# Five raw weight places instead of three in the second sweep of the first feed-forward layer, in the room of values that come later, and the work beside it spread over more tiles

## The chip, the core and the metric

The kernel runs on one core of a Trainium2 chip. The metric is the device time of one execution in microseconds. Before the change three runs gave 2960.24, 2964.97 and 2967.89 us; the median is 2964.97 us. The engines are named as in the profile: PE multiplies matrices, DVE works on vectors, ACT computes functions and copies, POOL is the general engine that also issues some of the DMAs here, SP issues the weight loads.

## The reference

A trunk of two layers works on 1024 latent tokens and 256 context tokens of width 1024. Layer 0 mixes tokens with a Conformer convolution module, layer 1 with grouped-query attention (16 heads, 4 key and value heads, head size 64, rotary positions on the latent tokens). A SwiGLU feed-forward of inner width 2816 follows each. What the change touches lies in the feed-forward of layer 0 and the start of layer 1:

```python
hx = rmsnorm(x, norm_g[i, 0]) * (1.0 + sc_x) + sh_x          # shift and scale from silu(c) @ w_mod
...
x = x + g_x * rmsnorm(yx, norm_g[i, 1])
fx = rmsnorm(x, norm_g[i, 2]) * (1.0 + scf_x) + shf_x
x = x + gf_x * rmsnorm(swiglu(fx, ffn_w1[i], ffn_w3[i], ffn_w2[i]), norm_g[i, 3])

def swiglu(h, w1, w3, w2):
    return (jax.nn.silu(h @ w1) * (h @ w3)) @ w2
```

In layer 1, `hx @ wq`, `hx @ wk` and `hx @ wv` give queries, keys and values, and the context tokens give keys and values of their own; queries and keys are normalised per head.

## The kernel before

All arithmetic is in float32. A product is computed from two halves of each operand: a value is rounded to a high half and the remainder is the low half, and three matmuls (high by high, high by low, low by high) are added in PSUM. So each weight block of 128 rows by 1024 columns takes three steps before PE can use it: SP loads it into a *raw place*, ACT rounds it into the high half (L144 or L161), and DVE subtracts to get the low half (L148 or L164). A raw place is free again once DVE has read it for the last time. The raw places are a list, `self.raws`, that `raw()` (L98) goes around. High and low halves have three buffers each (`wh`, `wl`).

The tokens stand in three pieces: C (256 context tokens), L and R (the two halves of the latent tokens, 512 each). The inner width 2816 is cut into 22 tiles of 128, in six groups of 4, 4, 4, 4, 3 and 3 (`GROUPS`).

The feed-forward of layer 0 is done in two sweeps over its weights. The first takes C and L together (L1347), the second R alone (L1393). `ffn` is a generator. For each tile it computes the two inner products and the product with silu (`up` or `up_fast`); after the first tile of a group it adds the down projection of the group before (`w2`, `down`: 96 matmuls of 512 columns for a group of 4); at the end `last` does the last group, with `evict` adding each result from PSUM to the sum in SBUF (L925) and `sq_acc` adding its square to a running sum (L389 on ACT, L390 on DVE).

In the second sweep all tiles but the first go through `up_fast` (L852). It computes a pair of 2 by 2 block products with seven block products instead of eight, each of four steps of three matmuls of 256 columns: 84 matmuls per tile. It takes two raw places for a tile (`r1`, `r3`, L859), issues their loads (L860, L861), and forms the sums and differences of the blocks in place on DVE (`tt`, L879), so that a place is in use from the start of its load until the last of its sums is split (L896). Three steps on ACT copy or silu partial results (L885, L898, L903), others add them on DVE (all L879).

Before the change the second sweep has three raw places: the two of the list, `wr0` and `wr1`, and `self.room()`, a tile named `q` (L1390). The second sweep of layer 1, which runs the same `up_fast` on R, has five.

Beside the second sweep runs a queue of background generators, `bgq`. After each step of the sweep, `pump` adds a credit, and generators run as long as the credit is above zero; each `yield` of a generator takes its cost off. The credit per unit of the sweep's work is set at L1401: 0.2 in the main part and 2.0 in the last group. The background does in this order (`early`, L1376): the last step of C and L of layer 0 (`final`, with its normalisation by L692 and L695), the norm of C into layer 1, keys and values of C (`qkv`, with `qk_pair`), eight steps of the norm of L; and then (`late`) the rest of the norm of L: the sums of squares added over partitions by PE (`stat`, L364), a reciprocal square root on DVE, its spread by PE transposes (L378), and eight applications, each of them L398 on DVE, L403 on ACT and L404 on DVE. Behind the sweep come keys, values and queries of L (`qkv`, L1405), the last step of R (L1409), its norm (L1411), its keys, values and queries (L1415), and attention.

Two large tiles matter for the change. `HR` has 5120 values per partition. During the second sweep its first part still serves C; from `qkv` of C on it holds the values of all heads and tokens (`self.vst`, L1380). Earlier in the kernel it holds inputs and the conditioning row (`cond_row`, L252).

The program is written in the order of these generators; a scheduler then orders the instructions of each engine by priority, which `later` lowers for a few (L362, L377), and each engine does its instructions strictly in that order.

Of the kernel before, what the change touches and what calls it, by code (L numbers as in the profile page):

```python
# [55 lines left out]
class Kern:  # L56
# [193 lines left out]
                                 bias=self.c["bmod"][:, 0, f:f + 1], scale=1.0)  # L250

    def cond_row(self, cr):  # L252
        self.nc.sync.dma_start(cr.rearrange("p s d -> p (s d)"), self.a["crow"].to_broadcast([P, 2048]))
        self.nc.scalar.activation(cr, cr, AF.Silu)

    def mod_dve(self, fs, cr, raws, junk):

        nc = self.nc

        def load(i):  # L260
            if i >= len(fs):
                return None
            raw = raws[i % len(raws)]
            if raw is None:
                raw = self.raw()
            nc.sync.dma_start(raw, self.a["wmodT"][0, fs[i]])
            return raw
        nxt = load(0)
        for i, f in enumerate(fs):
            raw, nxt = nxt, load(i + 1)  # L270
            for s in range(2):
                nc.vector.tensor_tensor_reduce(out=junk, in0=raw, in1=cr[:, s, :], scale=1.0, scalar=0.0,
                                               op0=ALU.mult, op1=ALU.add,
                                               accum_out=self.mod[0][s][:, f:f + 1])
                yield 1.13
        for s in range(2):
            m = self.mod[0][s][:, fs[0]:fs[-1] + 1]
            nc.vector.tensor_tensor(m, m, self.c["bmod"][:, 0, fs[0]:fs[-1] + 1], op=ALU.add)

    def mod_half(self, l, fs, cr, raws, junk):  # L280

        nc = self.nc
        part = self.cp.tile([P, 2, 48], F32, tag="mpart", name="mpart")

        def load(i):
            if i < 2 * len(fs):
                h = i % 2 * 512
                if self.tie is not None:
                    nc.scalar.copy(raws[i % len(raws)][:, 0:1], self.tie[:, 0:1].bitcast(F32))
                nc.gpsimd.dma_start(raws[i % len(raws)], self.a["wmodT"][l, fs[i // 2]][:, h:h + 512])  # L290
        ahead = len(raws) - 1
        for i in range(ahead):
            load(i)
        for i in range(2 * len(fs)):
            f, h = fs[i // 2], i % 2
            load(i + ahead)
            for s in range(1 if l and f >= 16 else 2):
                nc.vector.tensor_tensor_reduce(out=junk, in0=raws[i % len(raws)], in1=cr[:, s, h * 512:h * 512 + 512],
                                               scale=1.0, scalar=0.0, op0=ALU.mult, op1=ALU.add,
                                               accum_out=(part[:, s] if h else self.mod[l][s])[:, f:f + 1])  # L300
# [743 lines left out]
    def qkv(self, h, col0, n, wk, rope=None, highs=()):  # L1044
# [16 lines left out]
        for j in range(n // P):  # L1061
            out = self.bank("mm")
            self.mm3(out,
                     self.pairs(*h, j * P, (j + 1) * P),
                     lambda k: tuple(w[:, (k % 4) * 256:(k % 4 + 1) * 256] for w in wv[k // 4]),
                     KT, 256)
            jj = col0 // P + j
            ov = out[:, :256].rearrange("p (h d) -> p h d", d=HD)
            vh, vl = self.vst[:, :, jj, 0:HD], self.vst[:, :, jj, HD:P]
            nc.scalar.copy(vh, ov)  # L1070
            nc.vector.tensor_tensor(vl, ov, vh.bitcast(F32), op=ALU.subtract)
            yield 0.5
        if rope is not None:
            for t in range(NKV):
                def qsink(i, v):
# [6 lines left out]
                             qsink,  # L1082
                             self.rq[t][:, lat0 // P * 4:(lat0 + n) // P * 4])
                yield 5.0

    def load_k(self, t, kt, c0=0, c1=TOK):
        k = kt.bitcast(F32).rearrange("p (a t) -> p a t", a=2)
# [34 lines left out]
    def values(self, t, Ps, sums, dst, done):  # L1122
        nc, c = self.nc, self.c
        av = self.bank("av")
        for j in range(NJ):
            tp = self.bank("pt")
            for h in range(4):
                nc.tensor.transpose(tp[:, h * P:(h + 1) * P], Ps[h][:, j * P:(j + 1) * P], c["ident"])  # L1128
            ph, pl = self.ptring[self.ptslot % len(self.ptring)]
            self.ptslot += 1  # L1130
            nc.scalar.copy(ph, tp)  # L1131
            nc.vector.tensor_tensor(pl, tp, ph.bitcast(F32), op=ALU.subtract)  # L1132
            with self.later(self.lav):
                nc.tensor.matmul(av, lhsT=self.vst[:, t, j, :], rhs=ph, start=j == 0, stop=False)  # L1134
                nc.tensor.matmul(av, lhsT=self.vst[:, t, j, :], rhs=pl, start=False, stop=j == NJ - 1)  # L1135
            yield 0.87

        r = sums[:, 1, :]
# [46 lines left out]
    def build(self):  # L1185
# [3 lines left out]
        hs = {b: [] for b in PIECES}  # L1189

        nv = CG * OW
        hr = self.T("HR", [P, TOK + nv + 2 * 1024 + 256])
        cr = hr[:, TOK + nv:TOK + nv + 2048].rearrange("p (s d) -> p s d", s=2)
        xs = {"C": hr[:, :KT * CTX].rearrange("p (k n) -> p k n", k=KT), "L": self.T("T6", [P, KT, 512])}

        def load_x(b):
# [51 lines left out]
        self.u = hr[:, :TOK]  # L1248

        self.v = [hr[:, o:o + nv].rearrange("p (g n) -> p g n", g=CG) for o in (TOK, TOK + nv)]  # L1250
        self.vsum = hr[:, TOK + nv + 2048:TOK + nv + 2048 + OW]
        ut = self.T("HS", [P, 2, 2, CG, UW], F32R)
        self.u2 = [ut[:, i] for i in range(2)]
        kt = self.T("KB", [P, CG * UW + CG * NM * PH + 1024])
# [71 lines left out]

        def mods():

            cr = room[:, 2048:4096].rearrange("p (s d) -> p s d", s=2)
            raws = [room[:, o:o + 512] for o in (4096, 4608)]  # L1330
            q = self.room()
            raws += [q[:, :512], q[:, 512:]]
            self.cond_row(cr)
# [7 lines left out]
        def rest_R():  # L1341
            yield from pp("R")
            yield from mods()
        room = self.T("HR", [P, 5120])
        self.bgq.append(rest_R())
        fm, fg = [], None
        for i, us in enumerate(self.ffn(0, [(fv["C"][0], CTX), (fv["L"][0], 512)],  # L1347
# [75 lines left out]
    def attention(self, final, qr):  # L1423
# [50 lines left out]
        def out_proj(q0, otag, tags, ytag, box, xtag):  # L1474
# [18 lines left out]
            more = [self.acc(512), xr[:, KT, :]]  # L1493
            box += [more, xr]
            for k in range(KT):
                o = self.bank("mm")
# [219 lines left out]
```

## Time and profile before

| what | value |
|---|---|
| median of three runs | 2964.97 us |
| the profiled execution's own time | 2966.95 us |
| its span in the trace | 2965.2 us |
| PE busy | 2864.0 us, 97% of the span |
| DVE busy | 2159.8 us, 73% |
| ACT busy | 1331.8 us, 45% |
| PE's mean granted clock | 0.985 of full speed |
| moved by DMA | 336.58 MB, 114 GB/s on the mean |

The second sweep of layer 0 goes from 1071.6 to 1447.1 us, where `last` begins. The seam, as it is called below, goes from there to 1531 us, where the key projection of R begins. The second sweep of layer 1 goes from 2599.8 to 2940 us. PE's busy time is modelled from the starts of its matmuls, so a busy PE is not always a PE at full speed: a stage's length against the number of its matmuls says more. The granted clock is 1.00 at full speed. In rows of waits the columns are the waiting engine and line, what it waited for, then the sum in us, how often, and the longest.

### The profile page before, as it was taken

The numbers are of one execution on the slowest core, as the hardware profiler recorded it, in microseconds if no ns is written. First come the engines' busy times: TensorE is split into PE (matmuls) and PEld (weight loads), VectorE is DVE, ScalarE is ACT, GpSimd is POOL, SyncE is SP. The second block draws the span as 40 slices with busy tenths as digits, with TensorE's granted clock in tenths as the row PEclk, the third lists the DMA queues.
The fourth block names the chain that finished last, engine by engine and source line by source line (L and its number), as shares of the span: only waits on it lengthen the run. The fifth ranks groups of instructions, "written<-read, shape, count | busy, mean of one in ns | idle before, by whom it ended". The sixth has DMA issues, their size and how long they took to land.

```text
span 2965.2 us, 42721 instructions
## 1 busy us (share of the span) xinstructions
PE 2864.0 (97%) x16462; PEld 2452.4 (83%) x16462; DVE 2159.8 (73%) x3746; ACT 1331.8 (45%) x2227; POOL 222.5 (8%) x377
## 2 busy tenths in 40 slices
PE   8999989999999999999999999989999999999998
PEld 6888877888888888898888778767777778889997
DVE  6887787857555387776786899786676756787777
ACT  5222265532222244443444688645555543444444
POOL 0000001011122001000011111100010000010000
PEclk9999999999999999999999999999999999999999
DMA  6443444334355224333445211222223142343332
GB/s 246 133 124 97 122 129 166 114 119 135 125 168 175 66 84 152 100 102 96 138 153 172 88 45 45 93 84 82 63 77 85 56 149 93 114 162 109 103 100 76
DMA packets 131467, 336.58 MB, mean 114 GB/s; under 512 B 31296, under 2 KB 52832, under 8 KB 130112
## 3 DMA queue, kind: packets, MB, share of 16 engines
q1 hardware_dynamic: 77728, 222.33, 24.0%
q0 software_dynamic: 29344, 103.83, 10.7%
q10 hardware_dynamic: 24192, 7.70, 1.1%
q8 instruction: 129, 2.11, 0.3%
q14 instruction: 74, 0.61, 0.1%
HBM read 289.50 MB, written 38.93 MB: 111 GB/s over the span
## 4 chain that ended last, share of the span: by engine, by line
PE 83%; DVE 9%; DMA 3%; ACT 2%; issue 2%; ACTq 0%; POOL 0%; SPq 0%; DVEq 0%; POOLq 0%
PE ps L172 15%; PE ps L173 15%; PE ps L174 15%; PE ps L1110 4%; PE ps L1128 4%; PE ps L874 3%; PE ps L876 3%; PE ps L875 3%; PE ps L453 2%; PE ps L1134 2%; PE ps L455 2%; PE ps L454 2%; PE ps L1135 2%; PE ps L184 1%; PE ps L185 1%
## 5 line engine op out<-in xcount | busy, mean ns | idle before, releaser
L174 PE MATMUL ps<-T,wl 128*128 128x512 f32 (+1 forms) x1360 | 502.1, 369 | 3.0 <-DVE wl L148 3.0
L172 PE MATMUL ps<-T,wh 128*128 128x512 f32 (+1 forms) x1360 | 503.9, 371 | 0.9 <-DVE sm L838 0.4
L173 PE MATMUL ps<-T,wh 128*128 128x512 f32 (+1 forms) x1312 | 483.5, 369 | 0.0
L144 ACT CAST wh<-wr 128x1024 fp32r<-128x1024 f32 (+1 forms) x225 | 233.3, 1037 | 434.7 <-PE ps L173 323.7
L148 DVE TENSOR_TENSOR wl<-wr,wh 128x1024 fp32r<-128x1024 f32 (+1 forms) x225 | 271.5, 1207 | 175.2 <-ACT wh L144 173.8
L874 PE MATMUL ps<-T,wh 128*128 128x256 f32 x1092 | 313.3, 288 | 13.0 <-ACT wh L161 8.3
L876 PE MATMUL ps<-T,wl 128*128 128x256 f32 x1092 | 305.6, 283 | 2.3 <-DVE wl L164 1.9
L875 PE MATMUL ps<-T,wh 128*128 128x256 f32 x1092 | 306.9, 281 | 0.0
L1132 DVE TENSOR_TENSOR T<-ps,T 128x512 fp32r<-128x512 f32 x320 | 216.8, 687 | 108.2 <-ACT T L1131 107.4
L174 PEld LDWEIGHTS ps<-T,wl 128*128 128x128 f32 x1360 | 258.5, 190 | 43.7 <-DVE wl L148 3.3
L172 PEld LDWEIGHTS ps<-T,wh 128*128 128x128 f32 x1360 | 258.5, 190 | 43.2 <-ACT T L1498 1.7
L173 PEld LDWEIGHTS ps<-T,wh 128*128 128x128 f32 x1312 | 249.7, 190 | 38.1 <-DVE T L164 0.7
L1131 ACT CAST T<-ps 128x512 fp32r<-128x512 f32 x320 | 185.9, 585 | 192.3 <-PE ps L1128 178.5
L173 PE MATMUL ps<-HS,wh 128*128 128x512 f32 x656 | 256.7, 391 | 0.0
L172 PE MATMUL ps<-HS,wh 128*128 128x512 f32 x608 | 238.3, 392 | 1.6 <-ACT wh L144 1.6
L174 PE MATMUL ps<-HS,wl 128*128 128x512 f32 x608 | 237.3, 390 | 0.0
L874 PEld LDWEIGHTS ps<-T,wh 128*128 128x128 f32 x1092 | 206.6, 189 | 24.0 <-ACT wh L161 14.1
L876 PEld LDWEIGHTS ps<-T,wl 128*128 128x128 f32 x1092 | 205.8, 190 | 4.8 <-DVE wl L164 4.6
L875 PEld LDWEIGHTS ps<-T,wh 128*128 128x128 f32 x1092 | 207.3, 190 | 0.4
L1128 PE MATMUL ps<-cst,T 128*128 128x128 f32 x1100 | 190.2, 275 | 3.3 <-DVE T L1132 3.3
L1116 DVE TENSOR_SCALAR_CACHE_REDUCE T<-ps,rq 128x1280 f32<-128x1280 f32 x110 | 170.1, 1546 | 27.4 <-PE ps L1110 22.2
L1128 PEld LDWEIGHTS ps<-cst,T 128*128 128x128 f32 x1100 | 133.0, 141 | 49.9 <-DVE T L1132 31.0
(357 smaller groups left out, 6179.3 us busy)
## 6 DMA issues: line engine op xcount, KB each, us to landing
wr<-in_w SPq DMA_DIRECT2D x185, 512.0 KB, 3.6
wr<-in_pw SPq DMA_DIRECT2D x35, 512.0 KB, 3.6
q<-in_w SPq DMA_DIRECT2D x31, 512.0 KB, 3.7
HR<-in_wmodT POOLq DMA_DIRECT2D x56, 256.0 KB, 4.2
q<-in_wmodT POOLq DMA_DIRECT2D x56, 256.0 KB, 3.9
KB<-in_w SPq DMA_DIRECT2D x24, 512.0 KB, 3.6
q<-qsd POOLq DMA_DIRECT2D x32, 256.0 KB, 3.3
wr<-in_wo SPq DMA_DIRECT2D x16, 512.0 KB, 3.6
```

The costliest lines, as they stand in the source:

```text
L144: nc.scalar.copy(hi, raw)
L148: nc.vector.tensor_tensor(lo, raw, hi.bitcast(F32), op=ALU.subtract)
L172: nc.tensor.matmul(out[:, :n], lhsT=wh, rhs=xh, start=k == 0, stop=False)
L173: nc.tensor.matmul(out[:, :n], lhsT=wh, rhs=xl, start=False, stop=False)
L174: nc.tensor.matmul(out[:, :n], lhsT=wl, rhs=xh, start=False, stop=k == nk - 1)
L874: nc.tensor.matmul(out, lhsT=wh, rhs=bh, start=first and k == 0, stop=False, **skip)
L875: nc.tensor.matmul(out, lhsT=wh, rhs=bl, start=False, stop=False, **skip)
L876: nc.tensor.matmul(out, lhsT=wl, rhs=bh, start=False, stop=k == 3, **skip)
L1116: nc.vector.tensor_scalar(out=pt, in0=sc, scalar1=rq[:, h:h + 1], scalar2=None, op0=ALU.mult, op1=ALU.min, accum_out=mn)
L1128: nc.tensor.transpose(tp[:, h * P:(h + 1) * P], Ps[h][:, j * P:(j + 1) * P], c["ident"])
L1131: nc.scalar.copy(ph, tp)
L1132: nc.vector.tensor_tensor(pl, tp, ph.bitcast(F32), op=ALU.subtract)
```

## The change

`HR` shrinks from 5120 to 4096 values per partition, and a new tile `HV` has the other 1024, so the memory in use is the same. The values of the first two token tiles (the context's) go to `HV`, those of the others to `HR`, which `qkv` now claims only when the first latent value is computed, that is after the sweep. In the meantime the last 2048 values per partition of `HR` are two more raw places: the second sweep of layer 0 has five. They are taken off the list after it. The conditioning row, which lay in one piece, is loaded and put through silu in two halves, one of them in `HV`. The credits of the background beside the sweep go from 0.2 to 0.16 in the main part and from 2.0 to 0.65 in the last group. A scratch row of the output projection moves from one tile to `HV`.

```diff
     def cond_row(self, cr):
-        self.nc.sync.dma_start(cr.rearrange("p s d -> p (s d)"), self.a["crow"].to_broadcast([P, 2048]))
-        self.nc.scalar.activation(cr, cr, AF.Silu)
+        for s in range(2):
+            self.nc.sync.dma_start(cr[s], self.a["crow"][:, 1024 * s:1024 * s + 1024].to_broadcast([P, 1024]))
+            self.nc.scalar.activation(cr[s], cr[s], AF.Silu)
...
             jj = col0 // P + j
-            vh, vl = self.vst[:, :, jj, 0:HD], self.vst[:, :, jj, HD:P]
+            if jj >= 2 and len(self.vst) == 1:
+                self.vst.append(self.T("HR", [P, NKV, NJ - 2, P], F32R))
+            vh, vl = self.value(slice(None), jj)[:, :, 0:HD], self.value(slice(None), jj)[:, :, HD:P]
...
+    def value(self, t, j):
+        return self.vst[0][:, t, j, :] if j < 2 else self.vst[1][:, t, j - 2, :]
...
-        hr = self.T("HR", [P, TOK + nv + 2 * 1024 + 256])
-        cr = hr[:, TOK + nv:TOK + nv + 2048].rearrange("p (s d) -> p s d", s=2)
+        hr = self.T("HR", [P, KT * 512])
+        cr = [hr[:, TOK + nv:TOK + nv + 1024], self.T("HV", [P, 1024])]
...
-        self.vsum = hr[:, TOK + nv + 2048:TOK + nv + 2048 + OW]
+        self.vsum = hr[:, TOK + 2 * nv:TOK + 2 * nv + OW]
...
-            cr = room[:, 2048:4096].rearrange("p (s d) -> p s d", s=2)
-            raws = [room[:, o:o + 512] for o in (4096, 4608)]
+            cr = [room[:, 2048:3072], room[:, 3072:]]
+            raws = [half[:, :512], half[:, 512:]]
...
-        room = self.T("HR", [P, 5120])
+        room, half = self.T("HR", [P, 4096]), self.T("HV", [P, 1024])
...
-            self.vst = self.T("HR", [P, NKV, NJ, P], F32R)
+            self.vst = [self.T("HV", [P, NKV, 2, P], F32R)]
...
-        self.raws.append(self.room())
+        self.raws += [self.room(), room[:, 2048:3072], room[:, 3072:]]
...
-            self.pump((0.2 if i < FT + 4 * (len(GROUPS) - 1) else 2.0) * us)
+            self.pump((0.16 if i < FT + 4 * (len(GROUPS) - 1) else 0.65) * us)
+        del self.raws[3:]
...
-            xr = self.T(xtag, [P, KT + 1, 512])
+            xr = self.T(xtag, [P, KT if q0 else KT + 1, 512])
+            last = self.T("HV", [P, 512]) if q0 else xr[:, KT, :]
```

In the rows below, names are `output<-inputs` with buffer numbers, and the changed kernel's lines are shifted by one or two against those of before (L860 is L861, L364 is L365, L390 is L391, L398 is L399, L404 is L405, L925 is L926).

The first place is SP's queue in the second sweep, between the loads of the third and the fourth group of the down projection. Before, consecutive rows:

```order
L860 DMA wr0_73<-in_w1 128x1024
L861 DMA wr1_74<-in_w3 128x1024
L860 DMA q_8799<-in_w1 128x1024
L860 DMA wr1_74<-in_w1 128x1024
L861 DMA wr0_73<-in_w3 128x1024
L860 DMA wr0_73<-in_w1 128x1024
L861 DMA q_8799<-in_w3 128x1024
```

At the same place of the changed kernel:

```order
L861 DMA HR_4326<-in_w1 128x1024
L861 DMA wr1_74<-in_w1 128x1024
L862 DMA wr0_73<-in_w3 128x1024
L862 DMA q_8805<-in_w3 128x1024
L861 DMA HR_4326<-in_w1 128x1024
L143 DMA wr0_73<-in_w2 128x1024
L862 DMA HR_4326<-in_w3 128x1024
```

The loads are the same; the place that each goes into has moved from three names to five (`HR` stands for two of them).

The second place is DVE's order in the seam, at the end of the second sweep. `wl_12537` is the low half of the first latent key weight, `acc_12401` the running sum of squares of R, `T1` the sums of the down projection, and `T2` the low half of the norm of L. Before:

```order
L148 TENSOR_TENSOR wl_12537<-q_8799,wh_12536 128x1024
L390 TENSOR_TENSOR acc_12401<-acc_12401,sb_12423 128x512
L398 SCALAR_TENSOR_TENSOR sb_12426<-T5_4324,col100_7900,ps_72 128x512
L398 SCALAR_TENSOR_TENSOR sb_12430<-T5_4324,col100_7900,ps_72 128x512
L398 SCALAR_TENSOR_TENSOR sb_12434<-T5_4324,col100_7900,ps_72 128x512
L404 SCALAR_TENSOR_TENSOR T2_12381<-sb_12426,mod10_103,T3_12380 128x512
L404 SCALAR_TENSOR_TENSOR T2_12381<-sb_12430,mod10_103,T3_12380 128x512
L404 SCALAR_TENSOR_TENSOR T2_12381<-sb_12434,mod10_103,T3_12380 128x512
```

In the changed kernel the low half of the same weight is `wl_12543`, and it stands here:

```order
L399 SCALAR_TENSOR_TENSOR sb_12500<-T5_4328,col100_7906,ps_72 128x512
L391 TENSOR_TENSOR acc_12401<-acc_12401,sb_12497 128x512
L926 TENSOR_TENSOR T1_8806<-ps_72,T1_8806 128x512
L405 SCALAR_TENSOR_TENSOR T2_12427<-sb_12500,mod10_103,T3_12426 128x512
L399 SCALAR_TENSOR_TENSOR sb_12517<-T5_4328,col100_7906,ps_72 128x512
L391 TENSOR_TENSOR acc_12401<-acc_12401,sb_12514 128x512
L926 TENSOR_TENSOR T1_8806<-ps_72,T1_8806 128x512
L405 SCALAR_TENSOR_TENSOR T2_12427<-sb_12517,mod10_103,T3_12426 128x512
L399 SCALAR_TENSOR_TENSOR sb_12534<-T5_4328,col100_7906,ps_72 128x512
L391 TENSOR_TENSOR acc_12401<-acc_12401,sb_12531 128x512
L148 TENSOR_TENSOR wl_12543<-q_8805,wh_12542 128x1024
```

The low half of the key weight has moved from ahead of the applications of L's norm to behind all but the last step of them, and these now alternate with R's sums instead of standing in runs of three.

The third place is PE's order at the start of the latent key projection, where the matmuls of the sweep's last group end (`HS` is the inner product of R). Before:

```order
L185 MATMUL ps_72<-HS_8801,wl_12397 128x512
L183 MATMUL ps_72<-T3_12380,wh_12536 128x512
L184 MATMUL ps_72<-T2_12381,wh_12536 128x512
L185 MATMUL ps_72<-T3_12380,wl_12537 128x512
L183 MATMUL ps_72<-T3_12380,wh_12541 128x512
L184 MATMUL ps_72<-T2_12381,wh_12541 128x512
L183 MATMUL ps_72<-T3_12380,wh_12536 128x512
```

In the changed kernel:

```order
L185 MATMUL ps_72<-HS_8807,wl_12397 128x512
L183 MATMUL ps_72<-T3_12426,wh_12542 128x512
L184 MATMUL ps_72<-T2_12427,wh_12542 128x512
L183 MATMUL ps_72<-T3_12426,wh_12547 128x512
L184 MATMUL ps_72<-T2_12427,wh_12547 128x512
L172 MATMUL ps_72<-wh_12641,T3_12426 128x256 x2
L365 MATMUL ps_72<-cst_75,acc_12401 128x1 x4
L185 MATMUL ps_72<-T3_12426,wl_12543 128x512
```

The first matmul by a low half of a key weight has moved from third to behind all that doesn't need one, two matmuls of the value projection and the four of R's statistics among it.

More of the change, by code (lines that the diff above doesn't have):

```diff
@@ L271, in mod_dve @@
             for s in range(2):
-                nc.vector.tensor_tensor_reduce(out=junk, in0=raw, in1=cr[:, s, :], scale=1.0, scalar=0.0,
+                nc.vector.tensor_tensor_reduce(out=junk, in0=raw, in1=cr[s], scale=1.0, scalar=0.0,
                                                op0=ALU.mult, op1=ALU.add,
@@ L297, in mod_half @@
             for s in range(1 if l and f >= 16 else 2):
-                nc.vector.tensor_tensor_reduce(out=junk, in0=raws[i % len(raws)], in1=cr[:, s, h * 512:h * 512 + 512],
+                nc.vector.tensor_tensor_reduce(out=junk, in0=raws[i % len(raws)], in1=cr[s][:, h * 512:h * 512 + 512],
                                                scale=1.0, scalar=0.0, op0=ALU.mult, op1=ALU.add,
@@ L1133, in values @@
             with self.later(self.lav):
-                nc.tensor.matmul(av, lhsT=self.vst[:, t, j, :], rhs=ph, start=j == 0, stop=False)
-                nc.tensor.matmul(av, lhsT=self.vst[:, t, j, :], rhs=pl, start=False, stop=j == NJ - 1)
+                nc.tensor.matmul(av, lhsT=self.value(t, j), rhs=ph, start=j == 0, stop=False)
+                nc.tensor.matmul(av, lhsT=self.value(t, j), rhs=pl, start=False, stop=j == NJ - 1)
             yield 0.87
@@ L1488, in out_proj @@
             box.append((y, yacc))
-            xr = self.T(xtag, [P, KT + 1, 512])
+            xr = self.T(xtag, [P, KT if q0 else KT + 1, 512])
+            last = self.T("HV", [P, 512]) if q0 else xr[:, KT, :]
             for q in range(0, KT, 2):
                 nc.gpsimd.dma_start(xr[:, q:q + 2, :], self.x2d[:, q:q + 2, CTX + q0:CTX + q0 + 512])
-            more = [self.acc(512), xr[:, KT, :]]
+            more = [self.acc(512), last]
             box += [more, xr]
```

## The prediction

> **What bounds the kernel now.** The page comes first, for its shares of the span and for the chain of work that ended last.
>
> ```profile
> span 2965.2 us, 42721 instructions
> PE 2864.0 (97%) x16462; PEld 2452.4 (83%) x16462; DVE 2159.8 (73%) x3746; ACT 1331.8 (45%) x2227; POOL 222.5 (8%) x377
> PE 83%; DVE 9%; DMA 3%; ACT 2%; issue 2%; ACTq 0%; POOL 0%; SPq 0%; DVEq 0%; POOLq 0%
> ```
>
> PE bounds the kernel, but only 83% of the chain is PE: 9% is DVE and 3% DMA. So I asked for busy time by stage. The first row is layer 0's second sweep (the stage that changes), the next four are pieces of layer 1's second sweep, which runs the same code with five raw weight places, and the last three are the projection of the context keys inside layer 0's sweep and the two halves of the seam behind it. Columns: length, then busy time and instructions of PE, PEld, DVE, ACT and POOL, the granted clock, the DMA share, GB/s.
>
> ```profile
> 1071.60:1447.10 375.50, 358.28 (x2413) 326.94 (x2412) 289.03 (x495) 166.53 (x259) 16.86 (x28) 0.99 0.36 114
> 2622.00:2652.20 30.20, 28.51 (x230) 27.21 (x228) 29.91 (x49) 16.40 (x26) 2.75 (x5) 1.00 0.39 129
> 2652.20:2740.10 87.90, 87.90 (x561) 79.89 (x562) 60.89 (x87) 38.03 (x56) 4.61 (x7) 1.00 0.43 136
> 2718.30:2740.10 21.80, 21.80 (x99) 18.03 (x98) 13.55 (x19) 4.51 (x7) 0.00 (x0) 1.00 0.24 77
> 2740.10:2780.50 40.40, 40.40 (x338) 39.93 (x337) 33.61 (x50) 23.37 (x35) 0.00 (x0) 1.00 0.38 116
> 1222.40:1243.50 21.10, 17.92 (x134) 17.18 (x134) 13.07 (x28) 7.58 (x13) 1.45 (x2) 0.92 0.23 76
> 1447.10:1469.80 22.70, 18.14 (x72) 14.17 (x71) 21.13 (x32) 13.07 (x19) 3.07 (x5) 0.92 0.54 188
> 1469.80:1531.00 61.20, 55.97 (x307) 47.87 (x306) 46.14 (x84) 27.12 (x44) 9.55 (x16) 0.94 0.50 168
> ```
>
> Layer 1's rows give the unit prices of an unhindered sweep. Four fast tiles (84 matmuls each, 256 wide) take 40.40 us, so 10.1 us a tile and 0.12 us a matmul; one group of the down projection (96 matmuls, 512 wide) takes 21.80 us. Layer 0's sweep has 2413 matmuls: 21 fast tiles (1764), 4.75 groups of the down projection (456), half a group's worth for tile 0 (48), and 145 of the work beside it (96 for keys and values of the context, the rest smaller). By those prices: 21 × 10.1 = 212.1; 4.75 × 21.8 = 103.6; 0.5 × 21.8 = 10.9; 145 × 0.12 = 17.4 at most. The sum is 344.0 us; the stage took 375.5. So **31.5 us are lost in it**: 375.50 − 358.28 = 17.2 as idle PE, the others as half clock and matmuls that the trace stretches.
>
> What loses them is told by the chain of waits inside the sweep (start, length, what):
>
> ```profile
> 1159.30 1.24 DVE wl L164
> 1160.55 3.52 DMA q<-in_w
> 1164.17 0.69 DVE wr L879
> ...
> 1172.90 3.43 DMA wr<-in_w
> 1176.42 0.69 DVE wr L879
> ...
> 1184.82 3.58 DMA wr<-in_w
> 1188.42 0.69 DVE q L879
> ```
>
> For three tiles the chain leaves PE. It goes: DVE writes the low half of the last weights that a place holds (L164), the place is free, a load takes 3.4 to 3.6 us, DVE makes the sums of the next tile (L879), and again. The loads land 1164.1, 1176.4, 1188.4: one tile per about 12.1 us, where PE needs 10.1. With DVE's own part of a tile at 33.61/4 = 8.4 us (the row at 2740.10), 8.4 + 3.5 = 11.9 is that period. The transfers are not slow, they are started late:
>
> ```profile
> SPq L860 <- DVE wl L164: 93.8, 9, 18.1
> wr<-in_w SPq DMA_DIRECT2D x39, 512.0 KB, 3.7
> PE ps L874 <- ACT wh L161: 7.1, 15, 2.0
> PE ps L874 <- ACT sm L885: 3.8, 2, 2.6
> ```
>
> The first row is SP's queue: it sat at L860 for 93.8 us until DVE had let go of a place. The last two rows are PE's largest waits in the sweep. With three places and two taken per tile (`up_fast`, L859), only half of the next tile can be on its way.
>
> **The change part by part.**
>
> *Five places in the sweep.* SP's queue, shown above, tells what changes. Before, the same place comes back after two or three loads; now after about five, so a tile's two loads go out while the tile ahead of it is computed. The load leaves the cycle, which becomes max(10.1 PE, DVE's work). DVE's own part is 8.4, so 1.7 us of each tile is left to the work beside it, and 21.8 − 13.55 = 8.2 of each group.
>
> *The work beside it, spread.* DVE's 289.03 us split into 21 × 8.4 = 176.4 for the tiles, 4.75 × 13.55 = 64.4 around the groups, and 48 for the work beside. The room for it is 21 × 1.7 + 4.75 × 8.2 = 75, so it fits on the mean. Its transfers go through POOL's queue, whose engine is busy 16.86 us of 375.5, and not through SP's. It doesn't fit evenly: counting the new order's DVE rows by these durations (an estimate), the first four tiles hold 9.9, 11.7, 10.1 and 10.1 us, those between groups 8.7 to 9.7. I leave 3.5 us of loss there. Layer 1's own piece with such a surplus says the same: at 2622.0, DVE was busy 29.91 of 30.20 and PE lost 1.7.
>
> *What stays.* The projection of the context keys goes PE, DVE, PE, DVE, ACT, PE in a row; its order is the same in both kernels, and PE idles 21.10 − 17.92 = 3.2 us there and then runs at half clock:
>
> ```profile
> 1235.80:1239.20 3.40, 2.95 (x14) 2.89 (x14) 3.16 (x4) 1.55 (x3) 0.72 (x1) 0.50 0.60 165
> 1345.00:1348.40 3.40, 3.40 (x18) 3.40 (x18) 1.96 (x3) 1.32 (x2) 0.00 (x0) 0.50 0.37 106
> ```
>
> Such a 3.4 us window at 0.50 costs 1.7 us: 5 us stay. With 1.5 for the rest, 3.5 + 5 + 1.5 = 10 remain of 31.5, **a gain of 21.5 us**. These half-clock windows followed waits of at most 2.6 us (the longest of PE's in this sweep, above). [...]
>
> *The seam behind the sweep.* Here the credit falls from 2.0 to 0.65 a unit (L1401). Before, twelve of norm L's steps stand in one piece on DVE ahead of the sums that free PE's banks:
>
> ```profile
> 1455.33 2.06 DVE L398 SCALAR_TENSOR_TENSOR sb<-T,col,ps 128x512 f32<-128x512 f32 x3
> 1457.31 2.07 DVE L404 SCALAR_TENSOR_TENSOR T<-sb,mod,T 128x512 fp32r<-128x512 f32 x3
> 1459.30 2.06 DVE L398 SCALAR_TENSOR_TENSOR sb<-T,col,ps 128x512 f32<-128x512 f32 x3
> 1461.27 2.07 DVE L404 SCALAR_TENSOR_TENSOR T<-sb,mod,T 128x512 fp32r<-128x512 f32 x3
> 1463.26 1.28 DVE L925 TENSOR_TENSOR T<-ps,T 128x512 f32<-128x512 f32 x2
> PE ps L183 <- DVE T L925: 4.3, 1, 4.3
> ```
>
> That costs 4.3 + 1.7 of half clock = 6.0, and goes: after, DVE takes them in ones and twos between the sums. But the low half of the first latent key weight (`wl_12543`, made at L148) stood ahead of the twelve before, and stands behind them all now. In PE's order only four high-half matmuls, two of the value projection and four of R's statistics are left ahead of the first one that needs it (L185). What DVE does in this piece goes by these rows:
>
> ```profile
> L404 DVE SCALAR_TENSOR_TENSOR T<-sb,mod,T 128x512 fp32r<-128x512 f32 x7 | 4.9, 747 | 0.0
> L398 DVE SCALAR_TENSOR_TENSOR sb<-T,col,ps 128x512 f32<-128x512 f32 x7 | 4.9, 742 | 0.0
> L925 DVE TENSOR_TENSOR T<-ps,T 128x512 f32<-128x512 f32 x7 | 4.6, 686 | 0.9 <-PE ps L185 0.9
> L390 DVE TENSOR_TENSOR acc<-acc,sb 128x512 f32<-128x512 f32 x5 | 3.4, 685 | 0.0
> L148 DVE TENSOR_TENSOR wl<-q,wh 128x1024 fp32r<-128x1024 f32 x1 | 1.2, 1226 | 0.1
> ```
>
> From the first sum after norm L's statistics to the end of `wl_12543` it holds 8 of L398, 7 of L404, 6 of L925, 7 of L390 and the L148: 8 × 0.66 + 7 × 0.66 + 6 × 0.61 + 7 × 0.60 + 1.2 = 18.9 us (steps of a row of three follow each other every 0.66, as the starts 1455.33, 1457.31 and 1459.30 show; 0.60 stands for the shorter ones, from their means in proportion). The statistics (L364, L378) now stand in the last block itself, so this begins some 7.5 us after it starts (an estimate: about ten short DVE steps and the block's first sums lie ahead), and the low half is ready 26.4 us after. PE has the block's 72 matmuls, 0.75 × 21.8 = 16.4, and some 2.6 for those ten and the block's own statistics: 19.0. A **new wait of about 7 us at L185**, with half clock 1.7: 8.7 paid for 6.0 saved. On the other side R's statistics now follow the last sum at once, and the end of the seam is set by a chain (R's last step, its norm, its key projection) that starts there. I take +1.5, from −3 (that chain alone counts, and the old stall goes) to +6 (the stall of 7 stays whole and nothing comes back).
>
> *The rest.* The conditioning row comes in two loads and two Silu steps:
>
> ```profile
> L254 ACT ACTIVATE HR<-HR x2: 1909/1911/1913, 56.1 to 565.8; 128x2048 f32<-128x2048 f32 x2
> ```
>
> Two halves on an engine that is busy 45%: the second time, in layer 0's first sweep, they lie beside PE's matmuls; at 56 us, in the start-up, they cost between −1.9 and +1.9 (a whole step won or lost), taken as 0. The split value tile, the moved `vsum` and the `last` row of the output projection change where data lie, not how many instructions read them: 0.
>
> **Sum.** 2966.95 (this execution; its span is 2965.2) − 21.5 + 1.5 = 2947. That execution lies 2 us above the median 2964.97, so **2945 us**. The range: a gain from 9.5 to 31.5 in the sweep, and the seam's −3 to +6. What a measurement here can tell from no change is 0.3%, 8.9 us.
>
> **The rivals.**
>
> *DVE becomes the bound.* Were the slack in the groups of no use (their own work comes first), 48 us would meet 35.7 of slack in the tiles: 12 more stay lost beside the 10, a gain of 9.5: 2966.95 − 9.5 + 1.5 − 2 = 2957. For it: 29.91 of 30.20 in layer 1. Against it: the chain above, where DVE waited for three tiles' loads. 0.17.
>
> *All is won.* Layer 1's rows at 2652.2 to 2780.5 lose nothing; if layer 0 does likewise and the seam gives 3: 2966.95 − 31.5 − 3 − 2 = 2930. Against it: the key projection, unchanged. 0.13.
>
> *Nothing is won*, because SP's queue works in order and a load at L143 that waits holds the next tile's load behind it, so that the places stand empty. The seam alone counts: 2966.95 + 1.5 − 2 = 2966. Against it, in layer 1's sweep PE lost little by that line while SP waited even longer:
>
> ```profile
> SPq L143 <- DVE wl L164: 119.4, 22, 15.9
> PE ps L874 <- ACT wh L161: 1.2, 3, 0.4
> ```
>
> 0.07.
>
> *Slower by the seam.* If PE's wait for `wl_12543` is DVE's whole piece, the 18.9 us and 1.7 of half clock, and the low half of the second key weight, which follows, holds PE 1.2 us more, the seam costs 21.8 − 6.0 = 16 more than before and R's chain slides with it. It makes the kernel measurably slower only if the sweep gives back less than 16 − 8.9 = 7. At no gain: 2966.95 + 16 − 2 = 2981. Against it: DVE's and PE's work overlap in the block by the count above. 0.05.
>
> **How the numbers follow.** The forecast has 0.58. Faster than 8.9 us: the forecast, all won, and 0.10 of the DVE case: 0.81. Within: 0.07 of it and nothing won: 0.14. Slower: 0.05. The range 2933 to 2958 takes in the forecast, most of the DVE case, and part of "all is won"; left out are the rest of that, and the two cases above 2960.
>
> **What would show it.** Right: in the sweep's row PE's busy time close to its length, and the length near 354; no load of `in_w` in its chain; a wait at L185 of about 7 us for L148 at the seam and none at L183 for L925. Wrong: DVE above 95% busy over the tiles with PE idle (the DVE case); SP at L143 with PE waiting at L874 (nothing won); a wait over 15 us at L185 (slower); or time lost where I put nothing, at the start or in attention.

## The result, and the profile after

| | before | changed |
|---|---|---|
| median | 2965.11 us (2960.24 to 2967.89, 4 runs) | 2939.05 us (2938.3 to 2942.97, 4 runs) |
| ratio, 95% interval | | 0.9917 [0.9899, 0.9934] |
| span of the profiled execution | 2965.2 us | 2937.2 us |

The kernel became 26 us faster by the medians and 28.0 by the two traces; 2945 was forecast, in 2933 to 2958. The page of the changed kernel, its first lines and the chain by engine:

```profile
span 2937.2 us, 42731 instructions
PE 2847.7 (97%) x16462; PEld 2446.1 (83%) x16462; DVE 2160.7 (74%) x3746; ACT 1335.5 (45%) x2229; POOL 222.6 (8%) x377
PE 86%; DVE 7%; ACT 2%; issue 2%; DMA 2%; ACTq 0%; POOL 0%; SPq 0%; DVEq 0%; POOLq 0%
```

PE's share of the chain rose from 83% to 86%, DVE's fell from 9% to 7% and DMA's from 3% to 2%; DVE's busy time is the same (2160.7 against 2159.8). To see where the 28 us come from, both kernels are cut at the same matmuls: from tile 0 of the sweep to the last fast tile, from there to the latent key projection, the 70 us behind, and the 90 us behind those. Rows as in the prediction (length, busy time and instructions of PE, PEld, DVE, ACT, POOL, granted clock, DMA share, GB/s). Before:

```profile
1071.60:1435.49 363.89, 347.13 (x2328) 316.47 (x2327) 279.68 (x481) 159.98 (x249) 15.93 (x26) 0.99 0.36 113
1435.49:1469.83 34.34, 29.31 (x158) 24.64 (x157) 30.51 (x47) 19.64 (x30) 4.00 (x6) 0.95 0.50 169
1469.83:1540.00 70.17, 64.94 (x352) 55.34 (x351) 55.11 (x99) 31.68 (x51) 9.55 (x16) 0.95 0.44 146
1540.00:1630.00 90.00, 88.47 (x462) 75.71 (x462) 57.46 (x102) 40.60 (x59) 13.29 (x19) 0.94 0.55 169
```

Changed:

```profile
1072.29:1412.88 340.59, 335.31 (x2316) 311.41 (x2314) 280.70 (x469) 163.15 (x250) 15.97 (x26) 0.99 0.39 121
1412.88:1440.98 28.10, 28.08 (x171) 24.73 (x170) 23.62 (x48) 15.90 (x23) 2.89 (x4) 1.00 0.40 131
1440.98:1511.20 70.22, 61.96 (x327) 52.52 (x326) 53.89 (x96) 31.44 (x50) 10.65 (x18) 0.90 0.48 161
1511.20:1601.20 90.00, 88.82 (x475) 76.39 (x474) 63.24 (x110) 42.67 (x62) 13.14 (x19) 0.98 0.52 161
```

The sweep gave 363.89 − 340.59 = 23.3 us, the stretch behind it 34.34 − 28.10 = 6.2. The start cost 0.7 (1072.29 − 1071.60), and all that follows the start of the latent key projection took 0.8 more. That is 23.3 + 6.2 − 0.7 − 0.8 = 28.0.

The prediction draws the line elsewhere: its sweep includes the last fast tile, which ends at 1447.1 before and at 1423.0 now and takes 11.6 and 10.1 us. So 1.5 of the 6.2 belongs to the sweep, and 4.7 to the last group (22.7 us before, 18.0 now). By the prediction's line the sweep takes 1423.0 − 1072.3 = 350.7 us, where near 354 was forecast.

Inside the sweep, between 1158 and 1185 us of the changed kernel, the chain by line reads:

```profile
by line: PE ps L875 34.9%; PE ps L876 33.0%; PE ps L877 32.8%
```

Where it went through DVE and the loads before, it is matmul behind matmul, and in the whole sweep no load of `in_w` stands in the chain (before, 6.9% of the stage into `wr` and 1.9% into `q`); these tiles start at 1150.50, 1160.58, 1170.69 and 1180.81, every 10.1 us. SP's queue still waits for DVE nearly as long at the first load of a tile (91.1 us against 93.8), and most transfers take 3.6 us by the median (before, 3.7 into `wr` and 3.6 into `q`); the few into `q` take 4.5:

```profile
SPq L143 <- DVE wl L164: 124.3, 20, 16.6
SPq L861 <- DVE wl L164: 91.1, 9, 16.4
```

```profile
wr<-in_w SPq DMA_DIRECT2D x24, 512.0 KB, 3.6
HR<-in_w SPq DMA_DIRECT2D x21, 512.0 KB, 3.6
q<-in_w SPq DMA_DIRECT2D x10, 512.0 KB, 4.5
```

So the length of SP's waits told nothing by itself: what counts is whether PE waits behind them. PE's waits in the sweep that are left are those of the context keys' projection (0.7, then 2.0) and some of about 0.4:

```profile
PE ps L875 <- ACT wh L161: 3.3, 4, 2.0
PE ps L1030 <- DVE sm L1026: 0.7, 1, 0.7
PE ps L172 <- ACT wh L144: 0.4, 1, 0.4
```

At the seam, the changed kernel's waits between the last fast tile and 1450 us:

```profile
PE ps L172 <- DVE T L926: 3.9, 2, 2.1
PE ps L365 <- DVE acc L391: 1.3, 1, 1.3
PE ps L183 <- DVE T L926: 0.4, 1, 0.4
```

And what DVE did then, at the end of these:

```profile
1446.15 0.68 DVE L926 TENSOR_TENSOR T<-ps,T 128x512 f32<-128x512 f32 x1
1446.76 0.74 DVE L405 SCALAR_TENSOR_TENSOR T<-sb,mod,T 128x512 fp32r<-128x512 f32 x1
1447.42 0.74 DVE L399 SCALAR_TENSOR_TENSOR sb<-T,col,ps 128x512 f32<-128x512 f32 x1
1448.08 0.68 DVE L391 TENSOR_TENSOR acc<-acc,sb 128x512 f32<-128x512 f32 x1
1448.68 1.22 DVE L148 TENSOR_TENSOR wl<-q,wh 128x1024 fp32r<-128x1024 f32 x1
```

The new wait stands where it was forecast and has nearly the forecast size, 5.6 us in four pieces for 7 in one. It isn't booked to L148, though: the two value matmuls ahead of it needed a PSUM bank that DVE's sum (L926) had still to free, and R's statistics the last L391. When they were through, so was the low half.

### The profile page after: what moved, and what is told of

It reads as the page before. It is cut to its first block, busy times and chain, and to the rows that moved or that the text cites. A ratio compares the mean times of both kernels' runs of the same rounds, so it can differ in the third digit from the quotient of the medians.

```text
span 2937.2 us, 42731 instructions
## 1 busy us (share of the span) xinstructions
PE 2847.7 (97%) x16462; PEld 2446.1 (83%) x16462; DVE 2160.7 (74%) x3746; ACT 1335.5 (45%) x2229; POOL 222.6 (8%) x377
## 4 chain that ended last, share of the span: by engine, by line
PE 86%; DVE 7%; ACT 2%; issue 2%; DMA 2%; ACTq 0%; POOL 0%; SPq 0%; DVEq 0%; POOLq 0%
PE ps L172 15%; PE ps L173 15%; PE ps L174 15%; PE ps L875 4%; PE ps L877 4%; PE ps L876 4%; PE ps L1116 4%; PE ps L1134 4%; PE ps L1140 2%; PE ps L454 2%; PE ps L455 2%; PE ps L456 2%; PE ps L1141 2%; PE ps L185 1%; PE ps L183 1%
## 5 line engine op out<-in xcount | busy, mean ns | idle before, releaser
L172 PE MATMUL ps<-T,wh 128*128 128x512 f32 (+1 forms) x1360 | 502.5, 370 | 1.4 <-ACT T L161 0.8
L144 ACT CAST wh<-wr 128x1024 fp32r<-128x1024 f32 (+1 forms) x217 | 225.0, 1037 | 419.9 <-PE ps L173 307.2
L148 DVE TENSOR_TENSOR wl<-wr,wh 128x1024 fp32r<-128x1024 f32 (+1 forms) x217 | 261.9, 1207 | 168.5 <-ACT wh L144 167.1
L172 PEld LDWEIGHTS ps<-T,wh 128*128 128x128 f32 x1360 | 257.8, 190 | 43.7 <-ACT T L1506 1.7
L172 PE MATMUL ps<-HS,wh 128*128 128x512 f32 x608 | 238.4, 392 | 0.9 <-ACT wh L144 0.9
```

The source lines that it names most:

```text
L144: nc.scalar.copy(hi, raw)
L148: nc.vector.tensor_tensor(lo, raw, hi.bitcast(F32), op=ALU.subtract)
L172: nc.tensor.matmul(out[:, :n], lhsT=wh, rhs=xh, start=k == 0, stop=False)
```

## The experiments

Each kernel is an edit of the changed kernel; times are medians, with the kernel before on the same chip beside them, since that moved from 2965 to 2969 us between chips. The last two columns come from one trace of each kernel. How far two traces of the same program differ shows at the seam: the kernel with five places and doubled loads runs the changed kernel's program there, with the same waits, and took 1.6 us longer from its last fast tile to the 9000th matmul.

| kernel | us | before beside it | ratio, 95% interval | sweep to the last fast tile, us | last fast tile to latent keys, us |
|---|---|---|---|---|---|
| before | 2965.11 | | | 363.9 | 34.3 |
| changed | 2939.05 | 2965.11 | 0.9917 [0.9899, 0.9934] | 340.6 | 28.1 |
| five places, old credits | 2944.75 | 2968.71 | 0.9921 [0.9909, 0.9933] | 339.9 | 35.0 |
| three places, new credits | 2958.71 | 2968.71 | 0.9969 [0.9958, 0.9980] | 363.0 | 28.1 |
| 0.16 and 2.0 | 2942.86 | 2968.71 | 0.9915 [0.9903, 0.9927] | 341.6 | 33.3 |
| 0.2 and 0.65 | 2938.37 | 2968.71 | 0.9900 [0.9886, 0.9913] | 339.3 | 28.4 |
| 0.4 and 0.65 | 2943.81 | 2966.74 | 0.9929 [0.9913, 0.9946] | 348.0 | 29.8 |
| four places | 2938.74 | 2967.58 | 0.9910 [0.9895, 0.9925] | 340.5 | 30.7 |
| five, loads twice | 2940.45 | 2967.58 | 0.9913 [0.9896, 0.9929] | 340.3 | 28.1 |
| three, loads twice | 3001.94 | 2967.58 | 1.0123 [1.0107, 1.0140] | 400.3 | 30.2 |
| norm L's statistics early | 2941.39 | 2966.74 | 0.9917 [0.9902, 0.9931] | 342.0 | 26.7 |
| 0.2 and 0.65, context keys in pieces | 2934.32 | 2967.58 | 0.9891 [0.9875, 0.9908] | 336.6 | 28.4 |

**Five places alone.** The theory: the loads stood in PE's cycle, and the places alone take them out. The rival: DVE was the bound, and the thinner spread of the work beside gave the gain.

```diff
-            self.pump((0.16 if i < FT + 4 * (len(GROUPS) - 1) else 0.65) * us)
+            self.pump((0.2 if i < FT + 4 * (len(GROUPS) - 1) else 2.0) * us)
```

> Five raw places, the credits of before (0.2 and 2.0). Measured lengths of the sweep from tile 0 to the last fast tile: 363.9 us before, 340.6 in the changed kernel; from there to the latent key projection: 34.3 before, 28.1 changed. Theory (the loads were in the cycle, the places alone end that): the sweep takes 341 to 347 us and keeps at least three quarters of its 23 us, whatever the credit. Rival (DVE was the bound, and the thinner spread of the work beside gave the gain): 355 us or more. With norm L's statistics again in one run the seam is the open part: if twelve steps in one run are what stalls PE, it takes 31 to 34 us again. Whole kernel by the theory 2944 to 2952 us, by the rival 2957 to 2963.

**The credits alone.** The other half of the change:

```diff
-        self.raws += [self.room(), room[:, 2048:3072], room[:, 3072:]]
+        self.raws.append(self.room())
```

> Three raw places (the two of the list and the room), the credits of the changed kernel (0.16 and 0.65). Theory: the sweep to the last fast tile stays at 358 to 366 us, since the load is still in the cycle; only the seam is won: 2956 to 2962 us for the kernel. Rival (the spread gives the gain): the sweep takes 350 us or less, the kernel 2940 to 2950 us. If both are needed together, this run and the one with five places and old credits each lie near 2965.

The sweep's row with five places and the old credits, then with three places and the new ones:

```profile
1072.36:1412.27 339.91, 335.44 (x2316) 311.74 (x2314) 279.63 (x469) 163.56 (x250) 15.93 (x26) 0.99 0.39 121
```

```profile
1074.52:1437.47 362.95, 346.91 (x2328) 317.32 (x2326) 279.87 (x480) 160.03 (x248) 15.95 (x26) 0.99 0.37 114
```

In the sweep the two halves of the change don't mix: five places make it 340 us at either credit, three make it 363. In these four kernels the next stretch goes by the credits: 28 us with 0.65 at the end, 34 to 35 with 2.0. Both lengths with five places and old credits fell outside what was expected, the sweep below it (339.9) and the stretch above it (35.0). The rival falls. DVE is busy 280 us in all four. The gains of the whole kernel don't quite add up: 24.0 us by the places and 10.0 by the credits, each alone, and 26.1 together. With three places and the new credits PE has none of the changed kernel's waits at L172 (3.9 us); that this makes the difference is not shown.

**Is it the load's time?** If the load stands in the cycle, a load of twice the length must lengthen a sweep with three places and not one with five. Each weight load of a fast tile of layer 0 was issued twice into the same place, with five places and with three:

```diff
-            nc.sync.dma_start(r1, self.a["w1"][l, ft])
-            nc.sync.dma_start(r3, self.a["w3"][l, ft])
+            for _ in range(1 if l else 2):
+                nc.sync.dma_start(r1, self.a["w1"][l, ft])
+                nc.sync.dma_start(r3, self.a["w3"][l, ft])
```

> The changed kernel with each weight load of a fast tile of layer 0 issued twice into the same place, so that a place is filled after some 7 us instead of 3.5. Theory (with five places the load is out of the cycle): the sweep to the last fast tile takes 341 to 350 us, hardly longer. Rival (the transfers themselves are near their limit, and the places only hide part of it): 360 us or more.

> Three places, each weight load of a fast tile of layer 0 issued twice. Theory (the load stands in the cycle: free place, load, DVE): the period of a tile that follows a tile goes from about 12 to about 15 us, and the sweep to the last fast tile from 363 to 395 to 440 us. Rival (three places lose their 23 us by something else than the load's time, DVE's order or the split steps): 363 to 380 us.

The sweep with five places and doubled loads, with three and doubled loads, and the latter's chain for one tile:

```profile
1073.17:1413.44 340.27, 335.36 (x2315) 311.36 (x2314) 280.64 (x469) 162.93 (x250) 16.00 (x26) 0.99 0.56 181
```

```profile
1071.50:1471.75 400.25, 359.45 (x2328) 331.52 (x2326) 282.06 (x479) 163.76 (x249) 15.99 (x26) 0.93 0.50 156
```

```profile
1167.76 1.24 DVE wl L164
1169.02 3.36 DMA q<-in_w
1172.39 3.95 DMA q<-in_w
1176.36 0.70 DVE wr L881
...
1181.11 1.24 DVE wl L164
1182.36 4.73 DMA wr<-in_w
1187.11 4.31 DMA wr<-in_w
```

With five places 181 GB/s instead of 121 cost nothing (340.3 against 340.6). With three, the same loads cost 400.25 − 362.95 = 37.3 us: the chain shows the two transfers one behind the other between DVE's last read of a place and its next use. Of the 37.3, 24.8 are idle PE (40.8 against 16.0), the rest goes with a granted clock of 0.93 instead of 0.99. The theory is confirmed: with three places a load's length counts, with five neither its length nor the loads' rate does.

**How many places?** Four instead of five:

```diff
-        self.raws += [self.room(), room[:, 2048:3072], room[:, 3072:]]
+        self.raws += [self.room(), room[:, 2048:3072]]
```

> The changed kernel with four raw places instead of five in the sweep. Theory (a load leaves PE's cycle as soon as both places of the next tile can be filled while a tile is computed, which four places allow): the sweep to the last fast tile takes 340 to 346 us and the kernel 2938 to 2944. Rival (the down projection's loads, four per group, take the places of the next tile, so that the fifth is needed): 347 to 356 us, the kernel 2946 to 2956.

```profile
1071.96:1412.46 340.50, 335.24 (x2315) 311.50 (x2314) 280.81 (x469) 163.07 (x250) 16.01 (x26) 0.99 0.39 121
```

Four are enough for the sweep: two tiles of two places. The fifth is not needed there, not even around the down projections' loads. In the last group this kernel took 2.6 us longer (30.7 against 28.1), with a wait of 1.9 for L926, but no waits at L172 behind it; the whole is the same, 2938.74 us.

**The credits one by one.** The end's credit back at 2.0, and the main part's back at 0.2:

```diff
-            self.pump((0.16 if i < FT + 4 * (len(GROUPS) - 1) else 0.65) * us)
+            self.pump((0.16 if i < FT + 4 * (len(GROUPS) - 1) else 2.0) * us)
...
+            self.pump((0.2 if i < FT + 4 * (len(GROUPS) - 1) else 0.65) * us)
```

> The changed kernel with the credit of the last group back at 2.0. The sweep to the last fast tile should be 340.6 us as in the changed kernel. Theory (the lower credit there is what takes PE's 4.3 us wait away): the stretch from the last fast tile to the latent key projection goes from 28.1 to 31 to 34 us, the waits of 5.6 us behind it shrink, and the kernel takes 2940 to 2945 us. Rival (the order there does not matter, since the chain from the last step of R to its key projection sets the end): 2938 to 2940 us.

> The changed kernel with the credit of the main part back at 0.2. Theory (DVE has room enough at either credit): the sweep to the last fast tile takes 340 to 344 us and the kernel 2938 to 2943. Rival (0.2 puts too much beside a tile and DVE becomes the bound of the first tiles): 346 us or more, kernel 2945 or more.

The first: the sweep stays (341.6), the stretch behind takes 33.3 us with a PE wait of 3.8 at L183 again, as forecast. The second: the sweep takes 339.3, no longer than with 0.16, so the thinning from 0.2 to 0.16 gained nothing. PE's waits of this kernel in the seam, from its last fast tile to 1450 us, and the place of the first key weight's low half on its DVE:

```profile
PE ps L183 <- ACT T L404: 0.7, 1, 0.7
PE ps L184 <- DVE T L405: 0.5, 2, 0.3
```

```profile
1428.87 0.68 DVE L926 TENSOR_TENSOR T<-ps,T 128x512 f32<-128x512 f32 x1
1429.47 1.22 DVE L148 TENSOR_TENSOR wl<-q,wh 128x1024 fp32r<-128x1024 f32 x1
1430.61 0.74 DVE L399 SCALAR_TENSOR_TENSOR sb<-T,col,ps 128x512 f32<-128x512 f32 x1
```

Here the low half stands ahead of norm L's steps (1429.47; in the changed kernel 1448.68), PE's order is that of before, and the new waits of 5.6 us are down to 1.2. So this run also gives them a price, if a rough one: from the last fast tile to the start of the program's 9000th matmul, before took 159.2 us, the changed kernel 155.5, this one 153.5. The waits seem to cost some 2.0 us, not 7 and more, and 2.0 is hardly above the 1.6 by which two traces of the same order differ.

**More beside a tile.** Does the room on DVE that the prediction worked out (1.7 us a tile) exist as a limit at all? A credit of 0.4 in the main part, the end's at 0.65:

> The changed kernel with the credit of the main part at 0.4: twice the work beside a tile in the first half of the sweep, none in the second. Theory (a tile has 1.7 us of room on DVE, a group 8, and the work beside fits only if spread; at 0.2 the sweep took 339.3 us, no longer than at 0.16): here DVE bounds the first tiles, the sweep to the last fast tile takes 343 to 352 us, the kernel 2941 to 2950. Rival (five places let DVE run ahead so far that its spread does not matter at all): 338 to 341 us in the sweep, the kernel 2937 to 2939.

The sweep, and PE's waits in it up to 1200 us:

```profile
1069.80:1417.81 348.01, 338.56 (x2315) 314.81 (x2314) 281.01 (x469) 164.03 (x250) 15.93 (x26) 0.98 0.38 119
```

```profile
PE ps L877 <- DVE wl L164: 6.1, 1, 6.1
PE ps L875 <- ACT wh L161: 3.0, 2, 2.5
```

The rival of the prediction, DVE as the bound, is real: at 0.4 the sweep is 7.4 us longer than at 0.16, and its largest wait is one of 6.1 for DVE. It begins between 0.2 and 0.4.

**A miss: the statistics earlier.** I took the late start of norm L on DVE (its statistics in the last block) for the cause of the seam's new waits, and moved them one step ahead:

```diff
-            for _ in range(KT):
+            for _ in range(KT + 1):
                 yield next(gl)
```

> The changed kernel with one step more of the norm of L in the first part of the background: its sums over partitions, reciprocal root and transposes come inside the sweep and no longer in the last block. Theory (the four waits of 5.6 us at the start of the latent key projection come from that late start of norm L's steps on DVE): they fall to under 2 us, and the seam, from the last fast tile to 90 us past the first 70 of the key projection, gets 1 to 3 us shorter: kernel 2936 to 2938.5 us. Rival (they come from the applications being given out slowly, at 0.65): the waits stay at 4 us or more and the time at 2939.

PE's waits in its seam up to 1450 us:

```profile
PE ps L172 <- DVE T L926: 3.0, 1, 3.0
PE ps L185 <- DVE wl L148: 1.4, 1, 1.4
PE ps L183 <- DVE T L926: 0.4, 1, 0.4
```

4.8 us remain, and the time did not fall (0.9917 as before). That explanation is wrong. The rival, that the slow credit of 0.65 makes the waits, doesn't stand either: with 0.2 and 0.65 only 1.2 us were left. In this kernel, as in the changed one, the low half of the key weight stands behind norm L's steps and value matmuls stand ahead of it on PE; with 0.2 and 0.65 neither is so. Which of the two it takes, and why the scheduler puts it so, stays open.

**What was left, and a faster version.** The prediction left 5 us at the context keys. In this kernel their normalisation is given out in three pieces (a `yield 1.2` behind the sums of squares and one behind the transposes, in `qk_pair`, and 2.6 for 5.0 behind the whole), so that the next tile's steps stand ahead of it on DVE and ACT, with credits of 0.2 and 0.65:

```diff
                                      start=i == 0, stop=i == 1)
+        yield 1.2
         v = self.tiny([P, 16], "nv")[:, :4 * J]
...
+        yield 1.2
         if rq is None:
             nc.vector.tensor_tensor(EO, EO, pb[:, :n].unsqueeze(1).to_broadcast(both), op=ALU.mult)
```

> The changed kernel with credits of 0.2 and 0.65, and the normalisation of the context keys given out in three pieces over several tiles instead of in one. Theory (PE's waits of 0.7, 2.0 and 0.4 us there and the half clock behind them come from this chain standing ahead of the next tile's steps on DVE and ACT): these waits go, the sweep to the last fast tile takes 334 to 336.5 us against 339.3 with the same credits, the kernel 2931 to 2935 against 2938.4. Rival (the waits move to the next piece, or the half clock comes from elsewhere): 338 to 340 us in the sweep.

The three tiles and the down projection's part around it, with 0.2 and 0.65 alone and then with the pieces, both 312 matmuls:

```profile
1218.50:1260.74 42.24, 39.07 (x312) 38.15 (x311) 37.33 (x68) 25.31 (x43) 1.45 (x2) 0.96 0.36 112
```

```profile
1219.64:1258.97 39.33, 37.96 (x312) 37.03 (x311) 35.50 (x66) 25.07 (x43) 1.45 (x2) 1.00 0.38 121
```

2.9 us less, the clock back at 1.00, the wait of 2.0 gone; the sweep takes 336.6 us, 0.1 over what was expected. At 2934.32 us this has the lowest median here, 0.9891 of the kernel before; as whole kernels it and the one with 0.2 and 0.65 alone (0.9900) are not told apart, since their intervals overlap. DVE is now busy 35.50 of the piece's 39.33 us.

## Why the prediction was right, and where it was not

- **What bound the sweep: right.** The cycle "free place, load, DVE" was read off the chain, 8.4 + 3.5 us against PE's 10.1. The doubled loads show it in both directions: nothing lost with five places, 37.3 us with three.
- **The ideal of the sweep: right.** Without its last tile the sum was 344.0 − 10.1 = 333.9; the changed kernel took 340.6 and the faster version 336.6.
- **What stays: right in place, too large in size.** I left 10 us (3.5 in the first tiles, 5 at the context keys, 1.5 elsewhere); 340.6 − 333.9 = 6.7 stayed. The first two fast tiles took 11.84 and 10.77 us where the count of DVE's rows gave 9.9 and 11.7, some 1.5 lost instead of 3.5 beside their few extra small matmuls; the context keys cost PE its 3.2 us (20.24 − 17.07) and half clock again:

```profile
1249.76:1270.00 20.24, 17.07 (x112) 15.67 (x111) 13.69 (x30) 9.51 (x16) 1.45 (x2) 0.92 0.37 119
```

  By the prediction's line the gain in the sweep was 375.5 − 350.7 = 24.8 for 21.5.
- **The seam: wrong in sign.** The step that failed is "8.7 paid for 6.0 saved", taken as +1.5. The saving is there, if smaller: the last group took 22.7 us before and 18.0 now, 4.7 for 6.0. The new wait is there too, at 5.6 us, and the low half was being made at 1448.7 to 1449.9, 26 to 27 us after the last block began (its first matmul at 1423.0), as worked out. But it was charged as if everything behind it were full already. PE lost idle 70.22 − 61.96 = 8.3 us in the 70 us behind, against 5.2 before, and ran at 0.90 for 0.95; in the next 90 us it ran at 0.98 for 0.94. By length times one minus the clock, half clock costs 7.0 − 3.5 = 3.5 us more in the first stretch and 1.8 − 5.4 = −3.6 in the second. Net, from the start of the last group to the 9000th matmul, 147.5 us became 145.4: the seam gained 2.1 where it was to lose 1.5. So the step put too high a price on the new wait: all that lies between the latent key projection's start and the 9000th matmul took 4.7 − 2.1 = 2.6 us more, where 8.7 were charged for the wait and 1.2 of that taken back without a working. The chain through R, which was to bring time back, did not come earlier: R's key projection starts 86 us behind the last fast tile's end, 83 before, but PE has done 400 matmuls by then instead of 372. What spares the later half clock stays open. The value lies near the lower bound of −3 that was given for the seam. Another 1.8 us were gained behind the 9000th matmul, which no term of the sum names and which is within the scatter of the runs.
- **The clock: right.** The sum let the half clock at the context keys stay. Behind gaps of 0.7 and 2.0 us there in the changed kernel the clock fell again (0.50 from 1258.4 to 1261.8), and where the 2.0 went (the faster version) it stayed at 1.00 and the piece became 2.9 us shorter than with 0.2 and 0.65 alone (39.33 against 42.24, granted clock 0.96).
- **DVE as the bound: not here, but close.** At 0.16 and 0.2 there is room (340.6 and 339.3 us in the sweep), at 0.4 there isn't (348.0).
- **Nothing won, by SP's order: refuted.** SP's waits at the first load of a tile stayed nearly as long (91.1 us against 93.8), and those at L143 for DVE grew (124.3 us against 71.6), and PE no longer waited behind them.
- **The rest: right.** The start came out 0.7 us longer, and kernels that start alike differ by more (the sweep begins at 1069.8 to 1074.5 us in the traces with the two halves). No loss shows behind the seam.

## What to carry to other kernels

When the chain of waits leaves the bound engine for "buffer free, load, prepare" and the period is the sum of a load and the preparation, count the buffers in tiles: here two whole tiles' worth (four places) took the load out and a fifth added nothing. A doubled load is a cheap proof: here it cost 37.3 us where the load stood in the cycle and nothing where it didn't. And price a new stall by the stretch that it stands in, up to a point that both kernels must pass: 5.6 us of waits at the seam came to some 2.

## What the runs showed of the hardware that was not expected

Doubling the weight loads of a stage raised its traffic from 121 to 181 GB/s and the DMA share from 0.39 to 0.56, and the median landing of these loads only from 3.6 to 4.1 us (into `wr0` and `wr1`; the row of the doubled loads below); the sweep's length changed by 0.3 us.

```profile
wr<-in_w SPq DMA_DIRECT2D x42, 512.0 KB, 4.1
```

The half clock that came with short gaps lasted longer at the seam than at the context keys. At the seam PE waited 0.35, 1.82, 2.07 and 1.34 us within 8 us, the last until 1448.8. In the 3.41 us up to 1446.11 it was busy for 0.35, and from there the granted clock was 0.50 for 10.24 us:

```profile
1442.70:1446.11 3.41, 0.35 (x1) 0.19 (x1) 3.41 (x6) 1.85 (x4) 0.00 (x0) 1.00 0.46 159
1446.11:1456.35 10.24, 8.12 (x23) 6.57 (x24) 6.71 (x9) 1.63 (x3) 1.06 (x2) 0.50 0.58 196
```

That is three times the 3.41 us at 0.50 seen behind the context keys (1258.38 to 1261.79), where PE had been busy for 1.04 of the 3.41 us ahead and its longest wait was 2.0. So in both places the clock fell with no wait of PE over 2.07 us just ahead; no run here tests whether short gaps add up or how much idle time it takes, and not every fall fits: at 1524.62 the clock fell to 0.50 for 3.41 us, though PE had been busy for 3.23 of the 3.41 us before.
